# A hybrid attention step on one core: query and key norms and the value split read the projection's PSUM bank, buffers of the written-out order are given back later, and its account assumes a longer way from engine to engine

## The chip, the cores and the metric

The kernel runs on one core of a Trainium2 chip. The core has TensorE (PE in the profile, its weight loads PEld), VectorE (DVE), ScalarE (ACT), GpSimd (POOL) and SyncE (SP), which here issues every DMA. The metric is the device time of one execution in microseconds; the time of the kernel before is the median of three runs, 2167.8 us.

## The reference

One layer of a decoder step for 2048 prompt tokens and 32 sample tokens of width 1024. The input is RMS-normalised and projected; two attention branches run on it and are merged with sigmoid gates:

```python
qa, ka, va, ga, qb, kb, vb, gb, ma, mb = mixer_inputs(x, norm_g, w_in, ...)
# qk_norm: per head of 64, y = a * rsqrt(mean(a*a) + EPS) * gain (* 1/8 for q)
# branch A: window 128, 8 query heads on 2 kv heads, sinks
# branch B: 3 groups of 8 heads, (window, dilation) = (128,1), (512,4), (2048,16)
s = einsum(q, k) + bias;  p = exp(s - max);  o = p @ v / sum(p)      # 128 queries x 128 or 256 keys
o_b = combine_dilations(outs, lses)                                   # weights from the denominators
ya = (o_a * silu(ga)) @ w_up_a;  yb = (o_b * silu(gb)) @ w_up_b
y = x + (sigmoid(ma) * ya + sigmoid(mb) * yb) @ w_out
```

The last rows of the normalised keys and of the values are outputs as well (`new_prompt_*`, `new_sample_*`).

## The kernel before

Every fp32 matmul is done as three fp16 matmuls on a high and a low part. The work has four stages. First the normalised input is transposed into `hT`, and the two merge gates are projected and put to DRAM. Then come the three dilation groups of branch B (3, 2, 1), each in 16 tiles of 128 tokens; then branch A in 16 tiles; then the up and output projections.

A tile of branch B has three projections (q, k, v), each 24 matmuls of 512 columns into one of five PSUM banks (0, 1, 2, 5, 6), a chain of steps behind each, and the attention:

- q and k: `q_chain` and `k_chain` call `norm` (L726). It copies the bank to SBUF on ACT (L730) and gives the bank back, squares on ACT (L738), sums on DVE (L740), takes the power on POOL (L743; for q also the gains, L747) and multiplies on DVE (L751). `parts` splits the product into fp16 halves with `split`: high on ACT (L303), low on DVE (L306 or L308). `turn` transposes them by DMA (issued at L167), and for k two DVE copies (L773, in `k_turn`) make a second layout. The first buffer named in `norm`'s calls as scratch (`qn`, `kn`) holds the squares and later the halves until the DMA has read them.
- v: `v_chain` copies the bank to `stV` on ACT (L999), then splits it into `VT`, two slots. Tiles whose rows are outputs (all 16 of group 3, four of group 2, one of group 1) store `stV` by DMA; their key rows go out of `stK` behind a product on POOL (L977).
- attention: `attend` starts one `unit` per pair of heads, or per two pairs where a tile has no previous block, so four or two units a tile. A unit is eight score matmuls (four per head pair) into PSUM bank 3 or 4 in turn, bias and maximum on DVE (L801), exponentials on ACT (L810, L815), the split into `Ps`, a DMA transpose into `PT`, and 12 value matmuls for each unit into bank 7. `finish` copies bank 7 to `Ut` (L1011), which a DMA stores.

There are 48 tiles of branch B; 27 of them have a previous block and so four units.

The order in which each engine gets its instructions is fixed when the program is written. The function runs a small account of time: `Clock` has one time for PE and a free time for each of ACT, DVE and POOL. Each chain is a generator that issues an instruction, adds an assumed duration with `use` (which returns the engine's free time plus `LAT`), and is resumed when that time has come. A `Lock` (L43) stands for a buffer: `get` waits in the account until the former owner has called `put`. `ck.come` is the account's time for the landing of the last DMA. On the chip each engine then works its list in order and waits by semaphores for what its next instruction needs; a wait of the account costs nothing there by itself, but moves what comes behind it. PE issues a projection in pieces of three matmuls, and between two pieces whatever has come due in the account.

Around the attention the account waits for these: `attend` starts when the tile's q and k are ready and the scores of the tile before are issued; a key's transpose is issued after the scores of the tile before; units of one tile follow each other at `PACE0`, or at `PACE` while the next tile's q is not ready.

Of the kernel before, what the change touches and what calls it, by code (L numbers as in the profile page):

```python
# [78 lines left out]
class Clock:  # L79
# [1 line left out]

    LAT = 110

    def __init__(self):
        self.now = 0.0
# [63 lines left out]
def hybrid_kernel(ctx, tc, xp, xs, ca, cb1, cb2, cb3, rel_bias, norm_gain, w_in, qga, kga, sinks, qgb, kgb,  # L151
# [541 lines left out]
    Ps = [cv(2, 512, dt=F16) for _ in range(2)]  # L693
    A_OP1 = cv.off
    Ut = cv(CW)
    stK, stV = cv(512), cv(512)
    A_OP0 = A_OP1 + 1024
    op = [arena[:, A_OP0:A_OP0 + 1024], arena[:, A_OP1:A_OP1 + 1024]]
    cv = Carve(A_OP0 + 1024)
    cb = cv(3, CW)  # L700
    SAMP = cv.off
    A_STV = A_OP1 + CW + 1024
    VTa = [x.rearrange("p a b -> p (a b)")[:, 640:].rearrange("p (a b) -> p a b", a=3) for x in VT]
    kv = kn[:, 128:384]

    sq_l, qn_l, kn_l, U_l, Ut_l, stK_l, stV_l, cb_l, fst_l = (Lock(ck) for _ in range(9))
    S_l, Sb_l, Ps_l, op_l = ([Lock(ck), Lock(ck)] for _ in range(4))
    PT_l = [Lock(ck) for _ in range(3)]
    unit_n = [0]
# [13 lines left out]
    start.scored = start.valued = start.finished = True  # L723
    start.biased = 4

    def norm(src, p0, n, nh, blk, scr, dst, gains=None, raw=None):  # L726


        if raw:
            A.activation(dst, src, AF.Copy)  # L730
            src = dst
            yield use("A", ta(nh * 64))
            raw[0].put()
            yield from raw[1].get()
        st = nst[p0:p0 + n, nrm_n[0] % 5]
        nrm_n[0] += 1
        s = scr[p0:p0 + n, :nh * 64]
        A.activation(s, src, AF.Square)  # L738
        yield use("A", ta(nh * 64))
        V.tensor_reduce(st[:, 0, :nh], heads(s), axis=AX.X, op=OP.add)  # L740
        V.tensor_scalar(st[:, 1, :nh], st[:, 0, :nh], 1.0 / 64, blk.epsc[p0:p0 + n], op0=OP.mult, op1=OP.add)  # L741
        yield use("V", tv(nh * 64) + 140)
        G.tensor_tensor(st[:, 2, :nh], st[:, 1, :nh], nhalf[p0:p0 + n].to_broadcast([n, nh]), op=OP.pow)  # L743
        f = use("G", 250 + 170 * nh)
        r = st[:, 2, :nh, None].to_broadcast([n, nh, 64])
        if gains is not None:
            G.tensor_tensor(heads(s), r, gains.to_broadcast([n, nh, 64]), op=OP.mult)  # L747
            f = use("G", tg(nh * 64))
            r = heads(s)
        yield f  # L750
        V.tensor_tensor(heads(dst), heads(src), r, op=OP.mult)  # L751
        yield use("V", tv(nh * 64))
# [16 lines left out]
    def k_turn(nh, dst, cur):  # L769
        x, y = (v[:, :, cur] for v in dst)  # L770
        yield from turn(x, kn, nh)
        for j in range(2):
            V.tensor_copy(y[64 - 64 * j:128 - 64 * j], x[64 * j:64 * j + 64])  # L773
            e = use("V", 33 * nh + 65)
        yield e

    def unit(t, y, n3, us, last):
# [43 lines left out]
        yield from PT_l[n3].get()  # L821
        pt = PT[n3]
        SP.turn(pt.rearrange("p b (a t) -> p (b a) t", t=P), Ps[y].rearrange("p b c -> p (b c)"))
        yield ck.come
        Ps_l[y].put()
        yield ck.now + 1800
        yield from cond(ck, lambda: t.v and t.prev.finished)
        for a, (x, u, j) in enumerate(hs):
            h = t.head(u, j)
            vc = (h if g else j) * 64  # L830
            o = bank[7][:, h * 64:h * 64 + 64]
            for n in range(nk):
                s = t.vslot(n if nk == 2 else cur)
                q = a * w + n * P
                ph, pl = (pt[:, z, q:q + P] for z in (0, 1))
                vh, vl = (t.VT[z][:, s, vc:vc + 64] for z in (0, 1))
                mm(o, ph, vh, n == 0, False, 27)
                mm(o, ph, vl, False, False, 27)
                mm(o, pl, vh, False, n == nk - 1, 27)
# [114 lines left out]
    def bcast_rows(row, n):  # L954
        return row[:, None, :].to_broadcast([n, 8, 64])

    def b_tile(g, t, tok, rows, nk, cur, last, par):
        t.g, t.nk, t.cur = g, nk, cur
        t.st = ast[:, par]
        t.QT, t.KT, t.VT = QT[(len(made) - 1) % 3], KT, VT  # L960
        t.head = lambda u, j: 2 * u + j
        t.vslot = lambda s: s
        prev = t.prev
        old = prev.prev and prev.prev.prev

        def q_chain(b):
            yield from sq_l.get()
            yield from norm(b.ap[:, :], 0, P, 8, blocks[f"q{g}"], qn, sq, GR[:, g % 2:g % 2 + 1], (b.lock, qn_l))
            yield from parts(qn, sq, 8, 1.0)
            sq_l.put()  # L970
            yield from cond(ck, lambda: old is None or old.scored)
            yield from turn(t.QT, qn, 8)
            qn_l.put()
            t.q = True

        def k_rows():
            G.tensor_tensor(heads(stK), heads(stK), bcast_rows(gk_row[:, g % 2], P), op=OP.mult)  # L977
            yield use("G", tg(512))
            SP.dma_start(rows[:, :512], stK)
            stK_l.put()  # L980
            t.kept = True

        def k_chain(b):
            yield from stK_l.get()
            yield from norm(b.ap[:, :], 0, P, 8, blocks[f"k{g}"], kn, stK, raw=(b.lock, kn_l))
            yield from parts(kn, stK, 8, 2.0 ** 11)
            if rows is None:
                stK_l.put()
            else:
                ck.spawn(k_rows())  # L990
            yield from cond(ck, lambda: prev.scored)
            yield from k_turn(8, t.KT, cur)
            kn_l.put()
            t.k = True

        def v_chain(b):
            yield from stV_l.get()
            blk = blocks[f"v{g}"]
            A.activation(stV, b.ap[:, :], AF.Copy, scale=2.0 ** -20 if rows is None else blk.c)  # L999
            yield use("A", ta(512, 1))  # L1000
            b.lock.put()
            yield from cond(ck, lambda: prev.valued)
            yield from split(VT[0][:, cur], VT[1][:, cur], stV, 1.0 if rows is None else blk.vs, 512)
            if rows is not None:
                SP.dma_start(rows[:, 512:], stV)
            stV_l.put()
            t.v = True

        def finish():
# [5 lines left out]
            def store():  # L1015
                yield e
                SP.dma_start(comb[g][tok], Ut)
                Ut_l.put()
                t.stored = True

            ck.spawn(store())
# [15 lines left out]
    sampB = samp_carve(A_STV, prod2=None)  # L1037
    cv = Carve(sampB["end"])
    KT.append(cv(8, 2, P, dt=F16))
    QT.append(cv(8, P, dt=F16))  # L1040
    sampA = samp_carve(SAMP, PT=A_PT, prod2=arena[:, A_SP:A_SP + 512],
                      Sr=arena[:, A_K + 1536:A_K + 1808])
# [311 lines left out]
    def a_tile(i, t, par):  # L1354
# [1 line left out]
        cur = i % 2  # L1356
        t.g, t.nk, t.cur = 0, 2 if i else 1, cur
        t.st = ast[:, par]
        t.QT, t.KT, t.VT = QT[1 - par], KTa, VTa
        t.head = lambda u, j: u + 4 * j  # L1360
        t.vslot = lambda s: (i if s == cur else i - 1) % 3
        t.ob = t.ga = t.gb = t.gs = t.cb = t.placed = False
        op_x = i % 2
        o = op[op_x]
# [22 lines left out]

        def q_chain(b):
            yield from sq_l.get()
            yield from norm(b.ap[:, :], 0, P, 8, blocks["q0"], qn, sq, GR[:, 0:1], (b.lock, qn_l))  # L1390
            yield from parts(qn, sq, 8, 1.0, True)
            sq_l.put()
            yield from cond(ck, lambda: prev.prev.scored)
            yield from turn(t.QT, qn, 8)
            qn_l.put()
            t.q = True
# [450 lines left out]
```

## Time and profile before

| | |
|---|---|
| median of 3 runs | 2167.8 us (2167.16 to 2171.36) |
| the profiled execution | 2170.46 us, of which its span in the trace is 2168.6 us |
| PE busy | 2029.2 us (94%) |
| DVE, ACT, POOL busy | 1386.0 us (64%), 1053.3 us (49%), 707.9 us (33%) |
| granted TensorE clock, mean | 0.979 |

By stages, from a view that sums busy time in given stretches:

| stretch, us | stage | length | PE busy | DVE busy | ACT busy | granted clock |
|---|---|---|---|---|---|---|
| 0 to 420 | gates | 420 | 394.94 | 219.32 | 140.03 | 0.99 |
| 420 to 1440 | branch B | 1020 | 952.51 | 701.15 | 657.02 | 0.98 |
| 1440 to 1840 | branch A | 400 | 358.95 | 346.59 | 221.36 | 0.96 |
| 1840 to 2168 | up and out | 328 | 322.78 | 118.97 | 34.92 | 1.00 |

PE's busy time counts a matmul from its start to a modelled end, so what is not busy is time in which PE stood still for a wait. A group of the page's list gives, behind the busy time, the idle time of the engine just before the group's instructions and what ended it; the view of waits lists the same pairs, longest first. Idle time of an engine other than PE matters only where PE in the end waits for it.

### The profile page before, as it was taken

The page shows a single profiled execution, that of the slowest core. Times are in us where ns is not written, and L with a number is a line of the kernel's source. Part 1 is how long each engine was busy: PE and PEld are TensorE (multiplying, and loading weights), DVE is VectorE, ACT ScalarE, POOL GpSimd, SP SyncE. Part 2 cuts the span into 40 slices and gives each one's busy share as a digit, 9 for nine tenths or more (in the row PEclk, how much of TensorE's full clock was granted, in tenths as well). Part 3 has the DMA queues.
Part 4 walks back from the last instruction along what each step waited for, and adds up shares of the span by engine and source line. Part 5 has one row for each costly group of instructions (what it writes and reads, how often), then busy time and mean ns, then how long its engine had stood idle before and what let it go on. Part 6 is the DMA issues. An engine that isn't in the chain of part 4 may idle for free.

```text
span 2168.6 us, 36145 instructions
## 1 busy us (share of the span) xinstructions
PE 2029.2 (94%) x13042; PEld 1135.8 (52%) x13042; DVE 1386.0 (64%) x3305; ACT 1053.3 (49%) x2526; POOL 707.9 (33%) x530
## 2 busy tenths in 40 slices
PE   6999999999999899898999999997899997999999
PEld 3555555666665455554544554544455555444464
DVE  5546662576754577773767885869788898642331
ACT  5432312555555667665776766765456555300000
POOL 1000000255632245541324552426655653220110
PEclk9999999999999999999999999999999998999999
DMA  7896571368879568978857878744434366332322
GB/s 225 175 300 230 203 269 57 115 175 201 217 174 264 139 134 203 215 157 228 218 113 151 168 167 160 172 102 107 79 82 108 96 176 175 110 107 88 115 85 93
DMA packets 528389, 344.34 MB, mean 159 GB/s; under 512 B 397585, under 2 KB 427762, under 8 KB 528210
## 3 DMA queue, kind: packets, MB, share of 16 engines
q1 hardware_dynamic: 528210, 342.04, 61.4%
q8 instruction: 102, 1.67, 0.3%
q14 instruction: 77, 0.63, 0.1%
HBM read 193.53 MB, written 62.43 MB: 118 GB/s over the span
## 4 chain that ended last, share of the span: by engine, by line
PE 59%; DVE 15%; DMA 12%; ACT 5%; issue 4%; SPq 2%; POOL 2%; DVEq 0%; POOLq 0%; ACTq 0%
PE bank L259 58%; DMA arena<-arena 7%; DVE arena L308 3%; DVE arena L773 2%; DMA out_dram<-arena 2%; DVE slot L473 2%; DVE arena L801 2%; ACT arena L815 2%; SPq L161 1%; SPq L167 1%; ACT slot L470 1%; DMA hT<-arena 1%; ACT arena L303 1%; DVE arena L751 1%; POOL nst L743 1%
## 5 line engine op out<-in xcount | busy, mean ns | idle before, releaser
L259 PE MATMUL bank<-slot,hT 128*128 128x512 f16 (+1 forms) x4992 | 1127.6, 377 | 8.0 <-ACT arena L730 4.5
L259 PEld LDWEIGHTS <-hT 128*128 128x128 f16 x4992 | 546.8, 113 | 436.5 <-issue 45.2
L259 PE MATMUL bank<-hT,slot 128*128 128x416 f16 (+4 forms) x2928 | 530.8, 342 | 17.7 <-DVE slot L473 3.8
L743 POOL TENSOR_TENSOR nst<-nst,nhalf 128x8 f32<-128x8 f32 (+2 forms) x136 | 232.4, 1710 | 773.9 <-DVE nst L741 704.6
L259 PEld LDWEIGHTS <-slot 128*128 128x128 f16 x2928 | 287.2, 99 | 251.1 <-DVE slot L473 11.1
L259 PEld LDWEIGHTS <-arena 128*128 128x128 f16 x4336 | 267.9, 99 | 283.1 <-issue 88.9
L259 PE MATMUL bank<-arena 128*128 128x64 f16 (+5 forms) x3746 | 269.9, 230 | 88.6 <-DVE arena L773 44.5
L815 ACT ACTIVATE arena<-arena,ast,inv 128x256 f32<-128x256 f32 (+1 forms) x512 | 283.8, 555 | 7.0
L308 DVE SCALAR_TENSOR_TENSOR arena<-arena 128x512 f16<-128x512 f32 (+1 forms) x292 | 221.6, 772 | 92.2 <-ACT arena L303 91.2
L303 ACT ACTIVATE arena<-arena 128x512 f16<-128x512 f32 (+2 forms) x395 | 231.3, 607 | 98.6 <-DMA arena<-arena 53.8
L1172 POOL TENSOR_TENSOR arena<-arena 128x512 f32<-128x512 f32 (+1 forms) x102 | 140.1, 1373 | 120.7 <-DVE arena L1215 101.4
L259 PE MATMUL bank<-slot,arena 128*128 128x512 f16 x768 | 167.9, 379 | 2.1 <-DVE slot L473 1.6
L473 DVE SCALAR_TENSOR_TENSOR slot<-slot,gsc 128x512 f16<-128x512 f32 (+1 forms) x144 | 107.3, 745 | 86.7 <-ACT slot L470 86.2
L730 ACT ACTIVATE arena<-bank 128x512 f32<-128x512 f32 x112 | 65.8, 589 | 173.4 <-PE bank L259 89.4
L643 ACT ACTIVATE arena<-bank,wst 128x416 f32<-128x416 f32 (+2 forms) x82 | 48.7, 597 | 190.5 <-PE bank L259 162.9
L470 ACT ACTIVATE slot<-slot,gsc 128x512 f16<-128x512 f32 (+1 forms) x144 | 98.1, 681 | 73.2 <-DVE slot L473 63.7
L303 ACT ACTIVATE arena<-arena,yk 128x512 f16<-128x512 f32 (+2 forms) x40 | 25.5, 638 | 201.1 <-POOL arena L1706 186.4
L1706 POOL TENSOR_TENSOR arena<-arena 128x512 f32<-128x512 f32 (+2 forms) x40 | 48.7, 1218 | 221.2 <-DVE arena L1692 201.7
L801 DVE CUSTOM_DVE_ANT_0 arena<-bank,bias 128x128 f32<-128x128 f32 (+1 forms) x296 | 87.4, 343 | 50.2 <-PE bank L259 48.9
L740 DVE TENSOR_REDUCE nst<-arena 128x8 f32<-128x512 f32 (+2 forms) x136 | 85.6, 630 | 42.3 <-ACT arena L738 41.6
L773 DVE COPY arena<-arena 64x1024 f16<-64x1024 f16 (+1 forms) x128 | 77.5, 605 | 54.0 <-DMA arena<-arena 52.3
L810 ACT ACTIVATE ast<-ast,ninv 128x2 f32<-128x2 f32 (+1 forms) x212 | 61.2, 289 | 102.6 <-DVE ast L801 101.7
(167 smaller groups left out, 1758.5 us busy)
## 6 DMA issues: line engine op xcount, KB each, us to landing
arena<-in_cache_b_kv_dram SPq DMA_DIRECT2D x144, 256.0 KB
slot<-in_w_in_dram SPq DMA_DIRECT2D x64, 512.0 KB
arena<-Qs SPq DMA_DIRECT2D x96, 256.0 KB
arena<-in_w_in_dram SPq DMA_DIRECT2D x16, 1024.0 KB
gates<-arena SPq DMA_DIRECT2D x78, 208.0 KB
comb<-arena SPq DMA_DIRECT2D x48, 264.0 KB
arena<-comb SPq DMA_DIRECT2D x48, 264.0 KB
arena<-gates SPq DMA_DIRECT2D x24, 512.0 KB
```

Source lines behind the costliest of these rows:

```text
L259: T.matmul(out, l, r, start=start, stop=stop)
L303: A.activation(hi, src, AF.Copy, scale=scale)
L308: V.scalar_tensor_tensor(lo, src, scale, hi, op0=OP.mult, op1=OP.subtract)
L470: A.activation(b.part(0, k), src, AF.Copy, scale=sc)
L473: V.scalar_tensor_tensor(b.part(1, k), src, sc, b.part(0, k), op0=OP.mult, op1=OP.subtract)
L730: A.activation(dst, src, AF.Copy)
L740: V.tensor_reduce(st[:, 0, :nh], heads(s), axis=AX.X, op=OP.add)
L743: G.tensor_tensor(st[:, 2, :nh], st[:, 1, :nh], nhalf[p0:p0 + n].to_broadcast([n, nh]), op=OP.pow)
L773: V.tensor_copy(y[64 - 64 * j:128 - 64 * j], x[64 * j:64 * j + 64])
L801: V.tensor_tensor_reduce(out=o, in0=i_, in1=b_, scale=1.0, scalar=-3e38 if g else sinkS[:, u, j:j + 1], op0=OP.add, op1=OP.max, accum_out= ...
L815: A.activation(e, e, AF.Exp, bias=nm[:, x:x + 1], scale=inv[:, g:g + 1], accum_out=l[:, x:x + 1])
L1172: G.tensor_tensor(sprod[:n], q, k, op=OP.mult)
```

## The change

`LAT` goes from 110 to 200 ns, so every chain of the account is resumed later. `norm` no longer copies: square and multiply read the PSUM bank, the scratch buffer's lock is taken before, and the bank is given back after the multiply. `v_chain` splits straight from the bank into one of three value slots (`V3` is the new one), scaled by a constant; only tiles with rows to store also copy the bank, into `Ut` instead of `stV`, which is gone. In the account `Ps`, `stK` and `Ut` are given back 1200 ns after the assumed landing of the DMA that reads them, and a key's two copies are issued 1200 ns after the assumed landing of its transpose. For the value matmuls the total wait after the landing stays 1800 ns, split into 1200 and 600.

```diff
-    LAT = 110
+    LAT = 200
...
-    def norm(src, p0, n, nh, blk, scr, dst, gains=None, raw=None):
-
-
-        if raw:
-            A.activation(dst, src, AF.Copy)
-            src = dst
-            yield use("A", ta(nh * 64))
-            raw[0].put()
-            yield from raw[1].get()
+    def norm(src, p0, n, nh, blk, scr, dst, gains=None):
+
...
         yield from turn(x, kn, nh)
+        yield ck.now + 1200
         for j in range(2):
...
-        yield ck.come
+        yield ck.come + 1200
         Ps_l[y].put()
-        yield ck.now + 1800
+        yield ck.now + 600
...
+    def v_at(z, s):
+        return V3[:, z] if s == 2 else VT[z][:, s]
...
         def q_chain(b):
             yield from sq_l.get()
-            yield from norm(b.ap[:, :], 0, P, 8, blocks[f"q{g}"], qn, sq, GR[:, g % 2:g % 2 + 1], (b.lock, qn_l))
+            yield from qn_l.get()
+            yield from norm(b.ap[:, :], 0, P, 8, blocks[f"q{g}"], qn, sq, GR[:, g % 2:g % 2 + 1])
+            b.lock.put()
...
             SP.dma_start(rows[:, :512], stK)
+            yield ck.come + 1200
             stK_l.put()
...
         def v_chain(b):
-            yield from stV_l.get()
-            blk = blocks[f"v{g}"]
-            A.activation(stV, b.ap[:, :], AF.Copy, scale=2.0 ** -20 if rows is None else blk.c)
-            yield use("A", ta(512, 1))
+            yield from cond(ck, lambda: prev.prev is None or prev.prev.valued)
+            yield from split(v_at(0, t.vn), v_at(1, t.vn), b.ap[:, :], 2.0 ** -20, 512)
+            if rows is not None:
+                yield from Ut_l.get()
+                A.activation(Ut[:, :512], b.ap[:, :], AF.Copy, scale=blocks[f"v{g}"].c)
+                yield use("A", ta(512, 1))
+                SP.dma_start(rows[:, 512:], Ut[:, :512])
+                ck.at(ck.come + 1200, Ut_l.put)
             b.lock.put()
-            yield from cond(ck, lambda: prev.valued)
-            yield from split(VT[0][:, cur], VT[1][:, cur], stV, 1.0 if rows is None else blk.vs, 512)
-            if rows is not None:
-                SP.dma_start(rows[:, 512:], stV)
-            stV_l.put()
             t.v = True
...
                 SP.dma_start(comb[g][tok], Ut)
-                Ut_l.put()
+                ck.at(ck.come + 1200, Ut_l.put)
```

`k_chain` of branch B and `q_chain` of branch A change as `q_chain` does above.

Because the account sets the order, the lists of all engines change. On PE, in the middle of group 1 (its sixth tile), this follows the last score matmul of the tile's first unit (bank_99 is PSUM bank 3, bank_100 is bank 4; hT and slot mark projections). Before:

```order
L259 MATMUL bank_99<-arena 128x256
L259 LDWEIGHTS hT_65
L259 MATMUL bank_102<-slot_70,hT_65 128x512
L259 LDWEIGHTS hT_65
L259 MATMUL bank_102<-slot_70,hT_65 128x512
L259 LDWEIGHTS hT_66
L259 MATMUL bank_102<-slot_70,hT_66 128x512
L259 LDWEIGHTS hT_65
L259 MATMUL bank_101<-slot_67,hT_65 128x512
```

Now:

```order
L259 MATMUL bank_99<-arena 128x256
L259 LDWEIGHTS hT_65
L259 MATMUL bank_102<-slot_70,hT_65 128x512
L259 LDWEIGHTS hT_65
L259 MATMUL bank_102<-slot_70,hT_65 128x512
L259 LDWEIGHTS hT_66
L259 MATMUL bank_102<-slot_70,hT_66 128x512
L259 LDWEIGHTS arena
L259 MATMUL bank_100<-arena 128x256
```

The second unit's scores now stand three projection matmuls behind the first unit's; before, nine projection matmuls and twelve value matmuls stood between.

On ACT, in the middle of group 3, from the square of one tile's k to the value copy (L730 is the copy from the bank, L738 the square, L810 and L815 a unit's exponentials, L303 the high halves, L999 the value copy, L1011 the copy of bank 7; wst marks scales). Before:

```order
L730 ACTIVATE arena<-bank_98 128x512
L738 ACTIVATE arena<-arena 128x512
L730 ACTIVATE arena<-bank_101 128x512
L738 ACTIVATE arena<-arena 128x512
L303 ACTIVATE arena<-arena,wst 128x512
L810 ACTIVATE ast<-ast,ninv 128x4
L815 ACTIVATE arena,ast<-arena,ast,inv 128x128 x4
L1011 ACTIVATE arena<-bank_103,wst 128x512
L303 ACTIVATE arena<-arena 128x8x64
L303 ACTIVATE arena<-arena 128x512
L999 ACTIVATE arena<-bank_102,wst 128x512
```

Now (L731 is the square, L804 and L809 the exponentials, L1013 the copy of bank 7, L1004 the copy of a value's rows):

```order
L1013 ACTIVATE arena<-bank_103,wst 128x512
L731 ACTIVATE arena<-bank_101 128x512
L804 ACTIVATE ast<-ast,ninv 128x4
L809 ACTIVATE arena,ast<-arena,ast,inv 128x128 x4
L731 ACTIVATE arena<-bank_102 128x512
L303 ACTIVATE arena<-arena 128x512
L804 ACTIVATE ast<-ast,ninv 128x4
L809 ACTIVATE arena,ast<-arena,ast,inv 128x128 x4
L1004 ACTIVATE arena<-bank_96,wst 128x512
```

The copies in front of the squares are gone, the squares read the banks, and the two units' exponentials stand closer together.

## Rows read from the trace of the kernel before

**Rows 1.** Busy time (instructions) by stretch: PE, PEld, DVE, ACT, POOL, clock, DMA.

```profile
420.00:1440.00 1020.00, 952.51 (x6499) 539.40 (x6499) 701.15 (x1733) 657.02 (x1645) 422.91 (x285) 0.98 0.76 178
1440.00:1840.00 400.00, 358.95 (x2711) 215.99 (x2709) 346.59 (x891) 221.36 (x603) 219.30 (x181) 0.96 0.48 116
```

**Rows 2.** PE's waits, 420 to 1440 us: us in total, times, longest us.

```profile
PE bank L259 <- DVE arena L773: 33.1, 26, 4.7
PE bank L259 <- DMA arena<-arena: 18.3, 17, 3.9
PE bank L259 <- DVE ast L801: 6.0, 4, 3.1
PE bank L259 <- ACT arena L730: 4.5, 1, 4.5
PE bank L259 <- ACT arena L999: 2.2, 1, 2.2
```

**Rows 3.** The same view, 1440 to 1840 us.

```profile
PE bank L259 <- DVE arena L773: 11.4, 6, 4.1
PE bank L259 <- DVE ast L801: 6.6, 3, 4.0
```

**Rows 4.** Timeline of PE in group 3: start us, length us, what.

```profile
577.66 0.61 PE L259 MATMUL bank<-arena 128*128 128x128 f16 x8
578.11 9.88 PE L259 MATMUL bank<-slot,hT 128*128 128x512 f16 x45
...
591.30 0.55 PE L259 MATMUL bank<-arena 128*128 128x128 f16 x7 [0.93 <-DVE arena L773]
```

**Rows 5.** Timeline of ACT, the same stretch.

```profile
573.27 0.64 ACT L738 ACTIVATE arena<-arena 128x512 f32<-128x512 f32 x1
...
584.14 0.60 ACT L730 ACTIVATE arena<-bank 128x512 f32<-128x512 f32 x1 [1.08 <-PE bank L259]
...
590.52 0.60 ACT L730 ACTIVATE arena<-bank 128x512 f32<-128x512 f32 x1 [5.11 <-DMA out_dram<-arena]
```

**Rows 6.** Timelines of DVE and SP, the same stretch.

```profile
578.30 0.29 DVE L801 CUSTOM_DVE_ANT_0 arena<-bank,bias 128x128 f32<-128x128 f32 x1 [0.99 <-PE bank L259]
...
588.96 2.29 DVE L773 COPY arena<-arena 64x1024 f16<-64x1024 f16 x2 [1.55 <-DMA arena<-arena]
592.74 0.69 DVE L751 TENSOR_TENSOR arena<-arena 128x512 f32<-128x512 f32 x1
...
584.51 3.24 SPq L167 DMA_TRANSPOSE arena<-arena  x2
```

**Rows 7.** Timeline of PE: first and last of five waits over 1.8 us for L773.

```profile
689.47 0.91 PE L259 MATMUL bank<-arena 128*128 128x128 f16 x7 [4.72 <-DVE arena L773]
...
1113.23 0.49 PE L259 MATMUL bank<-arena 128*128 128x256 f16 x3 [1.99 <-DVE arena L773]
```

**Rows 8.** PE by 5 us after the first of them: PE busy, clock, DMA.

```profile
690.00:695.00 5.00, 5.00 (x23) 0.57 0.80 235
695.00:700.00 5.00, 5.00 (x27) 1.00 0.45 124
```

**Rows 9.** ACT's waits, 420 to 1440 us.

```profile
ACT arena L730 <- DMA out_dram<-arena: 80.1, 13, 10.6
ACT arena L999 <- DMA out_dram<-arena: 24.0, 7, 10.3
```

**Rows 10.** Groups by form: count, busy us, mean ns of one, idle before.

```profile
L730 ACT ACTIVATE arena<-bank 128x512 f32<-128x512 f32 x112 | 65.8, 589 | 173.4 <-PE bank L259 89.4 <-DMA out_dram<-arena 80.1 <-issue 3.7
L801 DVE CUSTOM_DVE_ANT_0 arena<-bank,bias 128x256 f32<-128x256 f32 x128 | 48.6, 418 | 10.6 <-PE bank L259 9.6
```

**Rows 11.** One line's forms: ns min/median/max, first and last start.

```profile
L751 DVE TENSOR_TENSOR arena<-arena x64: 671/687/1757, 400.3 to 1784.3; 128x512 f32<-128x512 f32 x64
...
L751 DVE TENSOR_TENSOR arena<-bank,nst x8: 283/679/683, 433.9 to 1471.1; 32x512 f32<-32x512 f32 x7, 32x128 f32<-32x128 f32 x1
```

**Rows 12.** DVE's waits, 420 to 1860 us.

```profile
DVE arena L801 <- PE bank L259: 60.8, 57, 4.8
```

More of the change, by code (lines that the diff above doesn't have):

```diff
@@ L695, in hybrid_kernel @@
     Ut = cv(CW)
-    stK, stV = cv(512), cv(512)
+    stK = cv(512)
     A_OP0 = A_OP1 + 1024
@@ L701, in hybrid_kernel @@
     SAMP = cv.off
-    A_STV = A_OP1 + CW + 1024
+    A_STV = A_OP1 + CW + 512
     VTa = [x.rearrange("p a b -> p (a b)")[:, 640:].rearrange("p (a b) -> p a b", a=3) for x in VT]
     kv = kn[:, 128:384]
-    sq_l, qn_l, kn_l, U_l, Ut_l, stK_l, stV_l, cb_l, fst_l = (Lock(ck) for _ in range(9))
+    sq_l, qn_l, kn_l, U_l, Ut_l, stK_l, cb_l, fst_l = (Lock(ck) for _ in range(8))
     S_l, Sb_l, Ps_l, op_l = ([Lock(ck), Lock(ck)] for _ in range(4))
@@ L832, in unit @@
             for n in range(nk):
-                s = t.vslot(n if nk == 2 else cur)
+                s = n if nk == 2 else cur
                 q = a * w + n * P
                 ph, pl = (pt[:, z, q:q + P] for z in (0, 1))
-                vh, vl = (t.VT[z][:, s, vc:vc + 64] for z in (0, 1))
+                vh, vl = (t.value(z, s)[:, vc:vc + 64] for z in (0, 1))
                 mm(o, ph, vh, n == 0, False, 27)
@@ L959, in b_tile @@
         t.st = ast[:, par]
-        t.QT, t.KT, t.VT = QT[(len(made) - 1) % 3], KT, VT
+        t.QT, t.KT = QT[(len(made) - 1) % 3], KT
+        t.vn = (len(made) - 1) % 3
         t.head = lambda u, j: 2 * u + j
-        t.vslot = lambda s: s
+        t.value = lambda z, s: v_at(z, t.vn if s == cur else t.prev.vn)
         prev = t.prev
@@ L984, in k_chain @@
             yield from stK_l.get()
-            yield from norm(b.ap[:, :], 0, P, 8, blocks[f"k{g}"], kn, stK, raw=(b.lock, kn_l))
+            yield from kn_l.get()
+            yield from norm(b.ap[:, :], 0, P, 8, blocks[f"k{g}"], kn, stK)
+            b.lock.put()
             yield from parts(kn, stK, 8, 2.0 ** 11)
@@ L1039, in hybrid_kernel @@
     KT.append(cv(8, 2, P, dt=F16))
+    V3 = cv(2, 512, dt=F16)
     QT.append(cv(8, P, dt=F16))
@@ L1358, in a_tile @@
         t.st = ast[:, par]
-        t.QT, t.KT, t.VT = QT[1 - par], KTa, VTa
+        t.QT, t.KT = QT[1 - par], KTa
         t.head = lambda u, j: u + 4 * j
-        t.vslot = lambda s: (i if s == cur else i - 1) % 3
+        t.value = lambda z, s: VTa[z][:, (i if s == cur else i - 1) % 3]
         t.ob = t.ga = t.gb = t.gs = t.cb = t.placed = False
@@ L1389, in q_chain @@
             yield from sq_l.get()
-            yield from norm(b.ap[:, :], 0, P, 8, blocks["q0"], qn, sq, GR[:, 0:1], (b.lock, qn_l))
+            yield from qn_l.get()
+            yield from norm(b.ap[:, :], 0, P, 8, blocks["q0"], qn, sq, GR[:, 0:1])
+            b.lock.put()
             yield from parts(qn, sq, 8, 1.0, True)
```

## The prediction, made before the changed kernel was run

> **What bounds the kernel now.** I read the busy times by stretch first. In the 1020 us of branch B, PE is busy 952.5 us, DVE 701.2, ACT 657.0 [rows 1]: PE is the bound and stands still for 67.5 us. In branch A PE is busy 359.0 of 400 us and DVE 346.6; DVE is nearly as full, and 41 us of PE's time are idle. Next, PE's waits name what the idle time is made of. In branch B 33.1 us are for the two DVE copies of a key's transpose (26 times), 18.3 for transposes themselves (a unit's probabilities, mostly), 6.0 for the bias and maximum of an earlier unit, which still hold the score bank, and 6.7 for ACT's copies out of a projection's bank [rows 2]. In branch A the copies cost 11.4 and the score banks 6.6 [rows 3]. The gates and the last stage have 30 us of idle time between them, most of it at the start.
>
> Last I followed one tile of group 3 through the timelines, since its waits repeat. A key's square starts at 573.27 [rows 5]; its transpose is issued at 584.51, the copies start at 588.96 and PE resumes at 591.30 after 0.93 us of waiting [rows 4, 6]. Meanwhile ACT stood 5.11 us before the copy of the next key, for the DMA that stores the previous key's rows out of the same buffer [rows 5]; over branch B such waits are 80.1 and 24.0 us of ACT [rows 9]. A tile takes 18.3 us there, of which the wait is 0.93.
>
> **The change, part by part.** Numbers "in wide matmuls" are counted in the two orders (columns over 512); one takes 9.88/45 = 0.22 us [rows 4].
>
> *Key copies later.* Between the last score of a tile and the first of the next, the new order puts on average 75 instead of 66 wide matmuls in group 3, 66 instead of 59 in group 2 and 62 instead of 54 in group 1: 8 more, 1.8 us. The key's projection itself lies 164 instead of 96 wide matmuls ahead of its scores in group 1. Scores are what triggers the next key's transpose, so this distance is what the wait for the copies has to fit in. Five waits in branch B are longer than 1.8 us, 15.8 us together (from 4.72 down to 1.95, one of them 1.99) [rows 7]; they keep 15.8 - 5 x 1.8 = 6.8 us, the other 21 end. Gain 33.1 - 6.8 = 26.3 us. Bounds: 33.1 (all go), and 8, if the chain of keys itself has no more speed (below). I take 26, as 21 of the 26 waits are short. In branch A the distance is 67 and 68, so its 11.4 stay.
>
> *Bank copies gone.* 112 ACT copies of 589 ns, 65.8 us [rows 10], leave ACT, and 27 of the 48 value copies with them, as only 21 tiles store rows: 27 x 0.59 = 16 us, 82 of ACT's 1053 us. ACT is not the bound; this sits beside PE's work. On the path are the two waits of 4.5 and 2.2 us [rows 2]. What is late next there is the DVE multiply that now frees the bank: I take 5 of the 6.7. Bounds 0 and 6.7.
>
> *ACT no longer held by stores.* The 104 us in which ACT stood before a store's buffer [rows 9] fall on group 3 and the sample rows. With `stK` and `Ut` given back later, other work stands before the waiting instruction. Behind it waited exponentials and high halves of units, whose transposes PE waits for (18.3 us) [rows 2]. But the first unit of a tile gets less room: from its scores to its values 59 instead of 67 wide matmuls in group 1, the fourth 89 instead of 79. So between -18 and +15 us; I take -4, nearer to nothing, because the two pull against each other.
>
> *Score banks.* This is the price. Units of a tile follow each other closer: from unit 0 to unit 2, which needs the same score bank, 13 instead of 23 wide matmuls in group 1 and 13 instead of 19 in group 2, 2.8 us. DVE's first instruction starts 578.30 - 577.66 = 0.64 us after the scores [rows 4, 6], two of 418 ns follow [rows 10], so the bank is free after 1.5 us at the earliest, with 1.3 us to spare. DVE waited for the scores only 57 times of 212 units [rows 12]; in the others it was still at something else, an instruction of 0.7 to 0.8 us or two. 27 tiles with two such places are 54; if a third of them lose 0.7 us, that is 12.6. I take +12. Bounds: -6 (even the 6.0 us of today go, as DVE is eased) and +54 (1 us each).
>
> *Banks held through the norm.* In the example the copy starts at 584.14 and the multiply ends at 592.74 + 0.69, 9.3 us [rows 5, 6]; without the copy 8.7. In the new order the bank of q is written again within 59 wide matmuls (13 us) in twelve tiles, eleven at 50 to 59 (11 us and more) and one at 30 (6.6 us). The one loses 2, the others little: +4, bounds 0 and +15.
>
> *Multiplies and low halves from PSUM.* DVE's count is unchanged, 3172. The multiply from SBUF takes 671 to 1757 ns, median 687; the few from PSUM 283 to 683, median 679 [rows 11]. In branch B DVE has 319 us free [rows 1], so I count nothing; bounds -8 (what DVE's fullness in branch A may give) and 0. The Trainium skill, "SBUF — State Buffer", section "Who interferes with whom", says that a DVE instruction with two SBUF inputs blocks against a GpSimd instruction that reads SBUF, and one with a single SBUF input does not; the maximum of 1757 against 683 agrees. Against the change speaks the Trainium skill, "VectorE: DVE Perf Modes", section "Rules for kernel authors": work on matmul output runs in the slowest mode, or is copied to SBUF first if there is much of it; the medians of 687 and 679 show no such loss for these fp32 products, and by that rule too the sum would stay.
>
> *Clock.* After the 4.72 us wait the granted clock is 0.57 over 5 us, which is the level of 1.2 GHz for most of them, then 1.00 [rows 8]: some 2 us more. With fewer long waits I take -3, bounds -6 and +4.
>
> *Everything else.* `LAT` reorders the first 200 us and the change of branches as well; the number of transposes and loads before each chunk of gates stays about the same. Zero, bounds -10 and +12.
>
> Sum: -26 - 5 - 4 + 12 + 4 - 3 = -22 us. The profiled execution took 2170.5, so 2148; it stands 2.7 us above the median, so 2146 on the scale of the runs.
>
> **The rivals.**
>
> *Score banks decide (slower).* If DVE is late by more than its spare 1.3 us nearly every time, each of the 54 places costs. The other terms are -34, so it turns at 34/54 = 0.63 us a place; at 1 us a place the time is 2168 + 54 - 34 = 2188. For it: in 155 of 212 units DVE was not yet free when the scores came. Against it: DVE has a third of branch B idle, and the waits of today are 6.0 us in 4 places [rows 2].
>
> *Nothing is gained: the chain of keys is the bound.* There is one `kn`. From a key's square at 573.27 to the next key's at 590.52 + 0.60 are 17.9 us [rows 5], and a tile without its wait needs 18.3 - 0.9 = 17.4. Taking 0.6 us of copy out of this loop leaves 17.3, hardly under PE's need; order then moves the waits to other instructions (the bank's multiply, the copies), and of the 26 us about 8 remain. Sum -4: 2164. Against it: 5.11 us of that loop are the wait for the store, which a square no longer needs.
>
> *Everything fits.* Copies -33, ACT's waits -7, transposes -9, clock -6, DVE eased in branch A -8, score banks 0: -63, 2105.
>
> **How the numbers follow.** Forecast 0.50 (2130 to 2160 as its own range), everything fits 0.17, nothing gained 0.12, score banks 0.21. A measurement tells about 0.2%, 4.3 us, from no change. Faster takes the forecast, the large gain and a part of the third case (0.02): 0.69; same 0.09; slower the last case and a little of the third: 0.22. The range leaves out a tenth on each side: 2110 to 2184.
>
> **What would show it.** The list of PE's waits after: under 12 us for the key copies in branch B; 10 to 25 for the bias and maximum; none for a copy from a bank, and a few us for the norm's multiply; 15 to 25 for transposes. ACT 80 us less busy, with no long wait for a store. The multiply's mean at 0.7 us. The prediction is wrong if the waits for the key copies stay above 20 us, if the score banks cost over 35, or if the first 420 us or the change to branch A move by more than 12 us.

## The result and the profile after

The changed kernel takes 2142.1 us (median of 4 runs, 2139.7 to 2145.6), the kernel before 2167.5 beside it: ratio 0.9883, 95% interval 0.9862 to 0.9903, 25 us faster. The forecast was 2146. The profiled execution has a span of 2141.1 us; PE is busy 2018.8 us in it (2029.2 before) and idle for 122.3 (139.4). So 17 us of the gain are idle time that went, and 10 are matmuls that ran at a higher clock: the mean granted clock rose from 0.979 to 0.981.

Busy time by stretch after, columns as in [rows 1]:

```profile
0.00:420.00 420.00, 393.98 (x2182) 225.33 (x2183) 214.72 (x490) 134.43 (x218) 19.37 (x29) 0.98 0.65 199
420.00:1440.00 1020.00, 972.79 (x6756) 553.62 (x6755) 703.12 (x1817) 610.45 (x1577) 428.57 (x301) 0.98 0.77 181
1440.00:1840.00 400.00, 357.07 (x2641) 214.26 (x2639) 350.22 (x851) 207.07 (x554) 214.07 (x173) 0.97 0.51 118
```

In the middle stretch PE does 20 us more work than before in the same time, ACT 47 us less. In the first 420 us PE does 1 us less (394.9 before). What PE waits for in 420 to 1440 us of the kernel after, in the columns of [rows 2]; L767 are the key copies (L773 before), L744 the norm's multiply (L751), L795 the bias and maximum (L801), L1004 the value copy out of the bank:

```profile
PE bank L259 <- DMA arena<-arena: 11.5, 8, 3.2
PE bank L259 <- DVE arena L767: 11.2, 11, 2.6
PE bank L259 <- DVE arena L744: 9.7, 5, 5.0
...
PE bank L259 <- DVE ast L795: 1.8, 1, 1.8
PE bank L263 <- ACT arena L1004: 1.7, 1, 1.7
```

The key copies' 33.1 us are 11.2 and the score banks' 6.0 are 1.8; ACT's copies are down to one wait. New are 9.7 us for the multiply that now frees the bank. In 1440 to 1840 us, against [rows 3]:

```profile
PE bank L259 <- DVE arena L767: 8.6, 7, 4.4
...
PE bank L259 <- DVE ast L795: 2.6, 2, 1.9
```

ACT's list for 420 to 1440 us is headed by other things than in [rows 9]. No wait for `out_dram` is in it any more; these two, for DVE's multiply and for a transpose, stand near its head:

```profile
ACT arena L303 <- DVE arena L744: 49.8, 24, 6.5
ACT arena L731 <- DMA arena<-arena: 45.9, 23, 6.3
```

The multiply from the bank, forms as in [rows 11]:

```profile
L744 DVE TENSOR_TENSOR arena<-bank,arena x64: 677/684/694, 402.4 to 1751.2; 128x512 f32<-128x512 f32 x64
L744 DVE TENSOR_TENSOR arena<-bank,nst x56: 283/683/694, 412.9 to 1439.1; 128x512 f32<-128x512 f32 x48, 32x512 f32<-32x512 f32 x7, 32x128 f32<-32x128 f32 x1
```

The maximum is 694 ns where it was 1757. Of the 64 multiplies in the first row, which before had both operands in SBUF, the mean fell from 937 to 685 ns; the median hardly moved (687 to 684). The Trainium skill, "SBUF — State Buffer", section "Who interferes with whom", has it that a DVE instruction with two SBUF inputs contends with GpSimd's reads and one with a single SBUF input does not; the fall of the mean and of the maximum agrees with it.

On the surface nearly everything came out as forecast. The experiments show that the forecast's main reason was wrong.

### The profile page after: what moved, and what is told of

Read it like the earlier page. It is cut to its first block, busy times and chain, and to the rows that moved or that the text cites. A ratio compares the mean times of both kernels' runs of the same rounds, so it can differ in the third digit from the quotient of the medians.

```text
span 2141.1 us, 35927 instructions
## 1 busy us (share of the span) xinstructions
PE 2018.8 (94%) x13042; PEld 1134.0 (53%) x13042; DVE 1366.4 (64%) x3305; ACT 979.2 (46%) x2387; POOL 697.7 (33%) x530
## 4 chain that ended last, share of the span: by engine, by line
PE 61%; DVE 16%; DMA 9%; ACT 6%; issue 4%; POOL 2%; SPq 1%; DVEq 0%; ACTq 0%; POOLq 0%
PE bank L259 60%; DMA arena<-arena 5%; DVE arena L308 3%; ACT arena L809 2%; DMA UB<-arena 2%; DVE arena L795 2%; DVE slot L473 2%; ACT arena L303 1%; ACT slot L470 1%; DVE arena L767 1%; SPq L167 1%; PE bank L885 1%; SPq L161 1%; DVE fst L1475 1%; DVE nst L733 1%
## 5 line engine op out<-in xcount | busy, mean ns | idle before, releaser
L736 POOL TENSOR_TENSOR nst<-nst,nhalf 128x8 f32<-128x8 f32 (+2 forms) x136 | 218.7, 1608 | 795.7 <-DVE nst L734 433.9
L259 PE MATMUL bank<-arena 128*128 128x64 f16 (+5 forms) x3746 | 264.6, 229 | 46.0 <-DVE arena L767 19.8
L809 ACT ACTIVATE arena<-arena,ast,inv 128x256 f32<-128x256 f32 (+1 forms) x512 | 283.9, 555 | 7.0
L303 ACT ACTIVATE arena<-arena 128x512 f16<-128x512 f32 (+2 forms) x368 | 215.8, 607 | 132.3 <-DVE arena L744 84.8
L308 DVE SCALAR_TENSOR_TENSOR arena<-arena 128x512 f16<-128x512 f32 (+1 forms) x292 | 234.8, 820 | 63.3 <-ACT arena L303 62.6
L804 ACT ACTIVATE ast<-ast,ninv 128x2 f32<-128x2 f32 (+1 forms) x212 | 61.7, 291 | 149.5 <-DVE ast L795 148.7
L795 DVE CUSTOM_DVE_ANT_0 arena<-bank,bias 128x128 f32<-128x128 f32 (+1 forms) x296 | 87.3, 343 | 48.2 <-PE bank L259 47.9
L303 ACT ACTIVATE arena<-arena,yk 128x512 f16<-128x512 f32 (+2 forms) x40 | 25.5, 637 | 200.6 <-POOL arena L1711 185.9
L731 ACT ACTIVATE arena<-bank 128x512 f32<-128x512 f32 (+2 forms) x120 | 69.7, 587 | 96.7 <-PE bank L259 49.5
L1755 DVE SCALAR_TENSOR_TENSOR slot<-bank,sst,slot 128x512 f32<-128x512 f32 (+1 forms) x33 | 24.8, 751 | 125.5 <-PE bank L259 115.6
```

The lines of the kernel that those rows point to most:

```text
L259: T.matmul(out, l, r, start=start, stop=stop)
L303: A.activation(hi, src, AF.Copy, scale=scale)
L308: V.scalar_tensor_tensor(lo, src, scale, hi, op0=OP.mult, op1=OP.subtract)
L795: V.tensor_tensor_reduce(out=o, in0=i_, in1=b_, scale=1.0, scalar=-3e38 if g else sinkS[:, u, j:j + 1], op0=OP.add, op1=OP.max, accum_out= ...
L804: A.activation(nm[:, xs_], m[:, xs_], AF.Copy, scale=ninv[:, g:g + 1])
L809: A.activation(e, e, AF.Exp, bias=nm[:, x:x + 1], scale=inv[:, g:g + 1], accum_out=l[:, x:x + 1])
```

## The experiments

Each run was timed in 5 rounds beside the kernel before on the same chip; ratios are to that kernel. Theory 1 is the prediction's: the account's longer times put more matmuls between two tiles' scores, and so cover the key copies. Theory 2: reading the banks pays, because it relieves ACT and the banks.

**The parts of the account alone, on the kernel before.**

```diff
# lat_alone
-    LAT = 110
+    LAT = 200
# kturn_alone
         yield from turn(x, kn, nh)
+        yield ck.now + 1200
# waits_alone: the line of kturn_alone, and
-        yield ck.come
+        yield ck.come + 1200
         Ps_l[y].put()
-        yield ck.now + 1800
+        yield ck.now + 600
             SP.dma_start(rows[:, :512], stK)
+            yield ck.come + 1200
                 SP.dma_start(comb[g][tok], Ut)
-                Ut_l.put()
+                ck.at(ck.come + 1200, Ut_l.put)
```

> The kernel before with only the account's way from engine to engine at 200 ns. Between the last score of a tile and the first of the next its order has 65, 67 and 58 wide matmuls in groups 3, 2 and 1, where the kernel before has 66, 59 and 54 and the changed one 75, 66 and 62. Theory 1 (the distance between tiles' scores is what pays: it covers the key copies): the waits for the copies in branch B fall from 33 to some 22 us, time 2158. Theory 2 (the relief of ACT and of the banks pays): nothing of that is in this kernel, copies' waits stay at 30 or more, time 2168.

> The kernel before with only the key copies issued 1200 ns later in the account. Distances 70, 69 and 65, units of a tile close together (12 wide matmuls from unit 0 to unit 2 in group 1, 23 before). Theory 1: copies' waits in branch B at 10 to 14 us, time 2150, although ACT does all it did before. Theory 2: no relief of ACT, so no gain: 2166. If close units cost (12 us in the prediction), the waits for the bias and maximum are over 15 us here and the time is 2160.

> The kernel before with only the four later times (key copies, Ps, stK, Ut by 1200 ns). Distances 79, 59 and 55 in groups 3, 2 and 1. Theory 1: the copies' waits go in group 3 and stay in group 1, 33 to some 18 us, time 2154. Theory 2: ACT no longer stands before stores (104 us in branch B fall under 40), which shortens the units' way to their transposes: PE's waits for transposes fall from 18 to under 12 us; time 2158, with copies' waits unchanged.

Measured: 1.0105 (1.0083 to 1.0127), 1.0116 (1.0095 to 1.0137) and 1.0134 (1.0113 to 1.0156); 2199.7, 2203.4 and 2206.6 us. All three are slower, 23 to 29 us by the ratios, which neither theory had forecast, though the distance between tiles' scores grew in kturn_alone by 4, 10 and 11 wide matmuls in groups 3, 2 and 1. Theory 1 is refuted as far as it says that distance pays by itself. PE's waits in kturn_alone, 420 to 1440 us (L774 are the key copies, L1000 and L730 ACT's copies of a value and of a key or query out of the bank):

```profile
PE bank L259 <- DVE arena L774: 33.1, 16, 7.4
PE bank L259 <- DMA arena<-arena: 21.1, 15, 5.2
PE bank L259 <- ACT arena L1000: 13.7, 5, 7.6
PE bank L259 <- ACT arena L730: 8.9, 3, 6.1
```

The copies wait fewer times, 16 for 26, but as long in all, and ACT's copies cost 22.6 us in these two rows where they cost 6.7. In waits_alone ACT stands behind the stores for 127.8 us (104.1 before):

```profile
ACT arena L1001 <- DMA out_dram<-arena: 105.4, 18, 10.3
...
ACT arena L730 <- DMA out_dram<-arena: 22.4, 6, 7.8
```

**The bank reads alone.** The changed kernel with LAT 110 and every added wait undone: the lines of lat_alone and waits_alone the other way round, and

```diff
                 SP.dma_start(rows[:, 512:], Ut[:, :512])
-                ck.at(ck.come + 1200, Ut_l.put)
+                Ut_l.put()
```

> Norms and value split from the bank, with the old 110 ns and without the later times. Distances 68, 58 and 53, as in the kernel before. Theory 1: the copies' waits stay near 30 us, only the 6.7 us of PE's waits for ACT's bank copies go; 2162. Theory 2: ACT is 80 us less busy, and most of the gain of the whole change is here: 2148.

Measured: 0.9804 (0.9785 to 0.9823), 2134.9 us. The bank reads alone give more than the whole change does. Theory 2 holds so far, but does not yet say by what they pay.

**Parts of the account undone or enlarged in the changed kernel.**

```diff
# after_no_kturn
-        yield ck.now + 1200
# after_kturn2400
-        yield ck.now + 1200
+        yield ck.now + 2400
# after_units_spaced
-    PACE0, PACE = 2000, 4500
+    PACE0, PACE = 4500, 4500
# after_lat110
-    LAT = 200
+    LAT = 110
```

> The changed kernel without the 1200 ns before the key copies. Distances between tiles' scores 71, 63 and 54 wide matmuls in groups 3, 2 and 1 (changed kernel 75, 66, 62; before 66, 59, 54). Theory 1 (distance covers the copies): the copies' waits in branch B, 11 us in the changed kernel, rise to some 20, mostly in group 1; time 2150. Theory 2 (relief of ACT and banks): as the changed kernel, 2142.

> The changed kernel with 2400 ns before the key copies. Distances 76, 68 and 64, one or two more than in the changed kernel. Theory 1: copies' waits in branch B 11 to some 7 us, time 2138. Rival: the rest of these waits has other causes (transposes late behind loads), the time stays at 2142 or grows, since the banks are held longer.

> The changed kernel with PACE0 at 4500 as PACE, so that the units of a tile stand 25 wide matmuls from unit 0 to unit 2, not 13; the distance between tiles shrinks to 64, 51 and 50. Theory 1: the copies' waits come back, 30 us or more, time 2160. If the score banks cost in the changed kernel what the prediction gave them, 12 us come back here: 2148. If they cost nothing, as its 1.8 us of waits for the bias and maximum say, only the loss is left.

> The changed kernel with the old 110 ns from engine to engine. Distances 71, 64 and 62. Theory 1: copies' waits 12 to 16 us, time 2145. If the longer way pays by itself elsewhere (gates, branch A, DVE's other waits), 2155.

Measured: 0.9871 (0.9843 to 0.9899), 0.9957 (0.9940 to 0.9975), 0.9835 (0.9810 to 0.9859) and 0.9741 (0.9718 to 0.9765). Without its wait the key copies cost PE 10.8 us in 420 to 1440, with it 11.2, and the time is the same within the intervals: what the distance does there (PE's waits for transposes are 32.0 us without it, 11.5 with it, those for the multiply 1.7 and 9.7) adds up to nothing that can be measured. With 2400 ns the key copies do fall, to 2.7 us, but the value copies' waits rise from 1.7 to 11.6 us and the multiply's to 14.6, and the time is 0.7% longer. `LAT` is the surprise: 200 instead of 110 costs the changed kernel 1.4%, 31 us by the ratios (0.9883 to 0.9741; the medians, of two chips, are 24 apart). after_lat110 is the fastest version of the study: it beats the kernel before by 2.6% and the changed one by 1.4%. PE's waits there, 420 to 1440 us:

```profile
PE bank L259 <- DMA arena<-arena: 19.8, 13, 4.7
PE bank L259 <- DVE arena L767: 11.4, 7, 5.0
...
PE bank L259 <- DVE arena L744: 1.8, 2, 1.3
```

The multiply's 9.7 us are 1.8: the banks held through the norm hurt only in the order that LAT 200 makes. PE's clock took part, its busy time is 2010.0 us (2018.8). The loss lies early: ACT's last copy of bank 7 in group 3 (L1013) starts at 746.7 us in after_lat110 and at 770.1 in the changed kernel (765.9 before), the last of branch B at 1378.6 and 1400.3 (1431.8 before). So the changed kernel gains nothing up to the end of group 3. Its chain of work that ended last holds a lead: from 420 to 1440 us, 3.3% of it, 34 us, are stores into `UB`, out of a buffer of the samples' attention that ACT fills at L1256; in after_lat110 they are some 6 us. But after_no_kturn has some 2 us of them and is no faster than the changed kernel, so which of the places that LAT moves is to blame stays open.

Spaced units gave 2138.3 us, faster than every expectation, and at the edge of what the two intervals tell apart from the changed kernel; the copies' waits did not come back (10.3 us). Since the waits for the score banks are only 4.4 us in the changed kernel's whole run, they can't be the reason, and it stays open.

**What the bank reads relieve.** Two parts alone, and one kernel that has neither of them:

```diff
# stores_free
-            SP.dma_start(rows[:, :512], stK)
+            SP.dma_start(rows[:, :512], hT[0][:, 7, :1024].bitcast(F32))
-                SP.dma_start(rows[:, 512:], stV)
+                SP.dma_start(rows[:, 512:], hT[0][:, 7, :1024].bitcast(F32))
# norm_alone: the change's edits of norm, q_chain and k_chain
-            A.activation(dst, src, AF.Copy)
# value_alone: the change's edits of v_chain, v_at and V3, without the wait for Ut
-            A.activation(stV, b.ap[:, :], AF.Copy, scale=2.0 ** -20 if rows is None else blk.c)
+            yield from split(v_at(0, t.vn), v_at(1, t.vn), b.ap[:, :], 2.0 ** -20, 512)
```

> The kernel before with the two stores of a tile's kept key rows and value rows reading a constant part of hT in place of the buffers that ACT writes (what lands in the caches is therefore other data; bytes and destinations are the same). Every engine's instructions stand in the same order as before; only the waits of ACT's copies (80.1 us and 24.0 us in the old profile) for these stores go. Theory 2a (the bank reads pay because ACT's copies no longer stand behind the stores of the rows): at least half of the gain of the bank reads alone, ratio 0.990 or less, 2150 or less. Theory 2b (they pay because the chain from a projection to its transpose is shorter and the multiply is eased): PE waited only 6.7 us for those copies, so 0.996 to 1.000, 2160 to 2168. The DVE row L751 keeps its mean near 0.91 us in both.

> The kernel before with only the query's and key's norm reading the bank (112 ACT copies go, all waits of the account and the value part as before). Theory 2b: most of the 2.0% of the bank reads, ratio 0.983 to 0.988, PE's waits for the key copies down from 44.5 us to 25 to 32 us in the whole run, the multiply's mean near 0.69 us. Rival (the value copies, 27 fewer and no longer behind the stores of the value rows, carry it): 0.993 to 1.000, since a bank is held through a whole norm.

> The kernel before with only the value part reading the bank (27 of 48 ACT copies go, a third value buffer, rows staged in Ut), the norm's copies as before. Theory 2b: a small part, 0.993 to 1.000, PE's waits for the key copies near 44 us and the multiply's mean near 0.91 us. Rival (the values carry it): 0.980 to 0.990.

Measured: 0.9826 (0.9807 to 0.9844), 0.9780 (0.9762 to 0.9799) and 0.9974 (0.9960 to 0.9988); 2130.9, 2121.7 and 2161.7 us. stores_free is the decisive one. PE, DVE, ACT and POOL carry out the same instructions in the same order as before, SP issues its DMAs in the same order, and as many bytes are stored to the same places; what goes is the wait of ACT's copies for the stores. SP need not wait for the rows either before it issues the stores, but that had cost it only 0.7 us in 420 to 1440 us of the kernel before. Freeing ACT of the stores alone gives 38 us, 1.7%. PE's waits in it, 420 to 1440 us:

```profile
PE bank L259 <- DVE arena L773: 24.3, 26, 2.9
PE bank L259 <- DMA arena<-arena: 16.6, 16, 2.8
PE bank L259 <- DVE ast L801: 3.4, 2, 2.1
```

Set beside [rows 2], the 6.7 us for ACT's copies are gone, and so are 8.8 us from the key copies, 2.6 from the score banks and 1.7 from the transposes: waits that name DVE or a DMA, and went with ACT's holds. Over the whole run PE is idle 112.6 us instead of 139.4, and its clock is 0.984, which takes 9 us from its busy time.

How a store gets into a wait for DVE is told by the chain of work that ended last (followed back from the last instruction to what released it), in the kernel before, around the 4.72 us wait of [rows 7] (start us, length us, what):

```profile
678.15 5.28 DMA out_dram<-arena
...
683.51 0.60 ACT arena L730
684.11 0.52 ACT arena L738
...
684.65 0.70 DVE nst L740
...
685.51 0.76 DVE slot L473
...
686.29 0.73 ACT slot L470
...
687.05 0.75 DVE slot L473
...
687.81 0.42 DVE arena L773
688.25 1.18 DVE arena L773
...
689.47 5.29 PE bank L259 x24
...
707.72 4.64 DMA out_dram<-arena
...
712.45 0.60 ACT arena L730
...
713.09 3.15 PE bank L259 x7
```

Read it downwards. A store is issued at 678.15 and lands 5.28 us later. Only then does ACT copy the next key into the buffer (L730, 683.51) and square it (L738). DVE stood idle for nearly all of it (6.18 us), and behind its reduce of that square (L740) come, with weights for other blocks between, the copies of an earlier key's transpose (L773, 687.81), which have no wait of their own (DVE's timeline, two rows):

```profile
684.65 0.69 DVE L740 TENSOR_REDUCE nst<-arena 128x8 f32<-128x512 f32 x1 [6.18 <-ACT arena L738]
...
687.81 1.60 DVE L773 COPY arena<-arena 64x1024 f16<-64x1024 f16 x2
```

PE's wait is named after these copies, but its root is the store: in stores_free the same matmul does not wait at all. The next one, at 707.72, holds PE through L730 itself; between 690 and 695 us PE ran at a granted clock of 0.57 besides [rows 8]. One pair of ACT's copies, first before, then in stores_free, shows what one hold does to ACT (timeline, last brackets: idle before it and its releaser):

```profile
620.00 0.60 ACT L730 ACTIVATE arena<-bank 128x512 f32<-128x512 f32 x1 [0.37 <-PE bank L259]
...
632.13 0.60 ACT L730 ACTIVATE arena<-bank 128x512 f32<-128x512 f32 x1 [10.58 <-DMA out_dram<-arena]
```

```profile
615.89 0.60 ACT L730 ACTIVATE arena<-bank 128x512 f32<-128x512 f32 x1 [0.37 <-PE bank L259]
...
621.63 0.60 ACT L730 ACTIVATE arena<-bank 128x512 f32<-128x512 f32 x1 [4.18 <-PE bank L259]
```

From copy to copy it is 12.13 us before and 5.74 without the hold. PE gained nothing by this one: stores_free is 4.1 us ahead of the kernel before at 620 us and 3.7 at 650. Followed instruction by instruction through the two timelines, the seven holds from 459 to 591 us, 39 us in all, give back 7 us when they go, the eight of over 2 us from 632 to 998, 56 us, give 26, and the two at 1075 and 1096, 7 us, give 7.

Where a hold lies on the chain, the chain shows it. By line, 420 to 1440 us, before and then kturn_alone:

```profile
by line: PE bank L259 47.7%; DMA arena<-arena 11.6%; issue 4.7%; DMA out_dram<-arena 3.8%; ACT arena L815 3.4%; DVE arena L773 2.8%; DVE arena L308 2.6%; SPq L161 2.0%; SPq L167 2.0%; ACT arena L303 1.8%; DVE slot L473 1.7%; DVE arena L801 
```

```profile
by line: PE bank L259 40.4%; DMA out_dram<-arena 7.5%; DMA arena<-arena 7.0%; issue 6.7%; ACT arena L816 4.2%; ACT arena L303 2.9%; POOL nst L743 2.7%; DVE arena L308 2.7%; SPq L167 2.6%; SPq L161 2.3%; DVE arena L774 1.7%; POOL arena L1173
```

3.8% of 1020 us are 39 us for the stores, and freeing ACT of them gave 38. In kturn_alone they are 7.5%, 77 us; in lat_alone and waits_alone 5.5 and 7.4%. In stores_free and in the changed kernel the view names no store of rows.

value_alone leaves the keys' copies behind the stores, 104.9 us, and gains 6 us; norm_alone has 37.9 us left on the values:

```profile
ACT arena L730 <- DMA out_dram<-arena: 104.9, 14, 11.7
```

```profile
ACT arena L996 <- DMA out_dram<-arena: 37.9, 11, 7.0
```

norm_alone is 0.5% below stores_free (9 us, the intervals just apart), although its holds on the values are still on the chain, 2.3% of it, 23 us. So the shorter norm, the faster multiply or the other order give something beyond the stores; how much is not shown, since no run reads the norms from the bank with all stores out of the way. The two parts don't add up: 2.2% and 0.3% make 2.5%, together they give 2.0%. A row of ACT in bank_alone, then the same in after_lat110, may say why: the values now wait for the store of `Ut`, the combination's buffer, and the account's waits for these stores take that away:

```profile
ACT arena L1002 <- DMA comb<-arena: 22.8, 8, 6.2
```

```profile
ACT arena L1004 <- DMA comb<-arena: 4.2, 5, 1.3
```

**The main term once more, without the stores.** kturn_free is kturn_alone with the two stores of stores_free:

```diff
         yield from turn(x, kn, nh)
+        yield ck.now + 1200
-            SP.dma_start(rows[:, :512], stK)
+            SP.dma_start(rows[:, :512], hT[0][:, 7, :1024].bitcast(F32))
...
```

> The kernel of kturn_alone (before, with 1200 ns of account time between a key's transpose and its copies, PE, DVE, ACT and POOL in the same order as there) with the two stores of key and value rows reading the constant part of hT, as in stores_free; what lands in the caches is other data. Theory 2a (spacing lost 1.2% alone because it put PE in front of copies of ACT that stood behind the stores): the loss goes, ratio 0.978 to 0.987 as stores_free's 0.983, PE's waits for ACT's copies out of a bank from 28 us to under 5. Theory 1 in what is left of it (distance covers the key copies once ACT is free): 0.970 to 0.977. Rival (the later order costs by itself, whatever ACT does): 0.990 to 0.998, some 25 us above stores_free.

Measured: 0.9786 (0.9763 to 0.9810), 2126.9 us. The 25 us that the spacing cost on the old kernel are gone: they were ACT's copies behind stores. By the ratios kturn_free is 72 us below kturn_alone, where the chain gave the stores 77. PE's waits, 420 to 1440 us:

```profile
PE bank L259 <- DVE arena L774: 15.1, 10, 4.1
PE bank L259 <- DMA arena<-arena: 13.4, 8, 5.8
```

Now the distance does what Theory 1 said: the key copies fall from 24.3 to 15.1 us. Against stores_free the time is 4 us less by the medians and 0.4%, 9 us, by the ratios, and the intervals just touch. So the distance is worth some 4 to 9 us, if anything, and only once ACT is free.

## Why the prediction was right, and where it was wrong

The time and the range were right, the mechanism was not, and that the sum came out is luck: two errors cancelled. The bank reads are worth 43 us, not the few that the terms gave them, and `LAT` at 200 costs 31, not nothing; the other waits of the account give 14 (0.9804 to 0.9741). -43 - 14 + 31 = -26 us, the 25 measured but for rounding. These are the prices in this order; put on the old kernel alone, `LAT` costs 23 us and the waits cost 29.

*Key copies later, -26 us: the step that failed.* It took each wait named after the copies for a matter of distance between scores. The waits for the copies did fall, from 33.1 to 11.2 us, but mostly without distance: bank_alone, which keeps the distances of the kernel before to within two matmuls, has 18.6. Distance alone made the old kernel 25 us slower, did nothing measurable in the changed one, and gave some 4 to 9 us where no store is in the way. The reading that misled was [rows 7]: of the wait at 689.47 I kept a part because it was longer than the 1.8 us of new distance, and did not ask why DVE came late. The chain has the answer, and I read only one tile of group 3, where such a hold happened to cost nothing [rows 5].

*ACT no longer held by stores, -4 us.* That the holds cost time was right. The size was not: 38 us alone, on the old kernel. Nor was the means: `stK` and `Ut` given back later left ACT 127.8 us of holds in waits_alone (104.1 before), and it was the reads from the bank that took them away. The bound of -18 was the sum of the transposes' waits; the effect came mostly through others, and through the clock. Of the 104 us of holds, 75 lie before the end of group 3 and 29 before that of group 2, all behind stores of tiles' rows and none behind sample rows: stores_free, which frees the tiles' stores alone, has none left. How the 43 us of the bank reads divide between the stores and the shorter norm is not shown.

*Bank copies gone, -5 us.* The 6.7 us of PE's waits for them did go; ACT is 74 us less busy, forecast 82.

*Score banks, +12 us.* Not seen: 1.8 us are left of 6.0. That DVE is "still at something else" when scores come [rows 12] did not make it late for the bank.

*Banks held through the norm, +4.* Seen, 9.7 us, inside its bounds of 0 to 15; it comes with LAT 200.

*Multiplies from PSUM, nothing.* DVE is 22 us less busy with them (115.0 to 93.2); what of it reaches the time no run separates. DVE's count is unchanged, as forecast; the traces have 3305 instructions, not 3172.

*Clock, -3.* Mean 0.979 to 0.981, and the busy time of PE fell 10 us: undersized by 7.

*Everything else, nothing.* `LAT` alone is +23 on the old kernel and +31 in the changed one, well beyond the bound of 12.

Of the rivals none came. "Score banks decide" had the wrong place. "Everything fits" came near the version without LAT 200 (2105 against 2118), by the wrong terms. Of the stated signs, copies under 12 us, ACT 80 us less busy, no long wait for a store of rows and the multiply at 0.7 us came true or nearly so; the bias and maximum (1.8 us, forecast 10 to 25) and the transposes (11.5, forecast 15 to 25) came out lower. The signs that came true could not tell the two theories apart: both let the copies' waits fall.

## What to carry to other kernels

The name at a wait is that of the last link. Before a wait is priced, follow the chain back past it, through what stands in front of that link on its own engine; a buffer held by a store can show up as another engine's delay. When an engine with half its time free stands for a DMA, look whether the chain that ended last runs through that DMA: its share there was close to the price here in both pairs that differ in the stores alone (39 us for 38, 77 for 72), while the waits that named ACT's copies (6.7) and the sum of ACT's own (104) were not.

## What the runs showed of the hardware

The chain of the kernel before runs ten times through a 256 KB store of a tile's rows between 420 and 1440 us; from its issue to its landing such a store takes 2.4 to 5.3 us there. The hold of ACT can be longer than that, since the store must first be issued. The hold of 5.11 us before 590.52 [rows 5] shows it (timelines of POOL and SP):

```profile
583.80 1.67 POOL L977 TENSOR_TENSOR arena<-arena,gk_row 128x512 f32<-128x512 f32 x1 [0.63 <-DVE arena L308]
...
587.85 0.53 SPq L161 DMA_DIRECT2D out_dram<-arena  x1
```

POOL's product was done at 585.47. SP was then at the two transposes of [rows 6] until 587.75, and issued the store only behind them; ACT's copy started 2.67 us after the issue. So nearly half of this hold is SP's queue, not the store.

Freed of such holds, the same matmuls in the same order took 9 us less of PE's busy time, at a mean granted clock of 0.984 instead of 0.979.
